# A ring of expert weights under attention's early memory, with raw w_out in it, and the row sums of the state-space half moved ahead

## The chip, the cores and the metric

The kernel runs on one core of a Trainium2 chip. The core has five engines that run at the same time, each with its own list of instructions: TensorE (matrix products), VectorE, ScalarE, GpSimd and SyncE (which here only issues transfers). The time is device microseconds of one execution; the median of several executions counts.

## The reference

One block of a streaming encoder on 1024 tokens of width 1024, all in float32. A combined input projection feeds a state-space mixer and a stick-breaking attention; both outputs are normed, joined and projected; a routed mixture of 32 experts follows.

```python
h = rms_norm(x, g_mix)
u, q, k, v = split(h @ w_in)                    # 512 columns each, 8 heads of 64
y_ssm = s5_mixer(u, ...)                        # ends with y * sigmoid(y @ w_glu + b_glu)
y_att = stick_breaking_attention(rms_norm(q, g_q), rms_norm(k, g_k), v)
mixed = concat(rms_norm(y_ssm, g_ssm_out), rms_norm(y_att, g_attn_out))
x = x + mixed @ w_out                           # w_out: 1024 x 1024
h2 = rms_norm(x, g_ffn)
x = x + hierarchical_moe(h2, ...)               # group top 1, expert top 2; gate, up, down per expert
```

The norms divide each token's row by the root of its mean square, so the joined projection needs the sum of squares of every token over the 512 columns of each half.

## The kernel before, in words

**Stages.** The input projection and the state-space scan are interleaved. Then comes attention, then the output projection with the router's logits, then the experts. The state-space output lies transposed in `yT` (columns on the partitions, tokens along the row); after its gate it is called `zT`, in the same memory. Attention writes its output, also transposed, over `q_t`, where it is called `oT`.

**Attention** (L672 to L756) is 64 steps: four pairs of heads, eight blocks of 128 queries each, two heads per block. `att_a` computes the scores on TensorE (L688, L689, L692), their sigmoid on ScalarE (L693), one minus it on GpSimd (L694) and a scan along the keys on VectorE (L697). `att_b`, three steps later, transposes the weights on TensorE (L708) and copies them to `aT` on ScalarE (L712) or VectorE (L714). `att_c` multiplies by `v_t` (L721) and copies the result to `oT` on ScalarE (L723). `sb`, `bb` and `aT` are the buffers in between. Queries and keys of a pair are prepared in one of two sets: set 0 for pairs 0 and 2, set 1 for pairs 1 and 3.

**The work list** (L725) spreads the state-space gate over attention: every third step takes one entry. `glu_w` loads and splits the gate's weights, `glu_split` splits half of `yT`, `glu_n` computes one block of the gate; the last multiplication is L660. With the last entry the pool of the GLU tiles is closed. `pair_prep` runs among these steps too.

**The seam.** After attention, `w_out` (1024 x 1024) is loaded in eight pieces of 512 KB into a buffer `wor` that is two deep (L794), scaled and split into a high part `wh` on ScalarE (L795) and a low part `wl` on VectorE (L796). `row_ss` (L800 to L817) takes the row sums of one half: for each 512 tokens, four squares on ScalarE (L806) and four products with a 128 x 32 matrix of ones on TensorE (L807), each into its own strip of 32 partitions of one bank, a copy (L809), four transposes (L812) and a reduction (L813); then the inverse root. It runs for `zT` and for `oT`, both after attention by the program, though the order of an engine's list may differ from it.

**The output projection** runs over eight tiles of 128 tokens. The left operand is split as well (`mh` L87, `ml` L88); each pair of parts gives three products (L91 to L93) of 128 x 128 by 128 x 512, 48 per tile. When a tile is done, its rows are normed and transposed for the router (L1012).

**Memory.** Tiles are placed in pools on the left or the right side of a partition's memory, one behind the other. A pool that opens where a closed one lay takes over its memory, and each tile waits until the last reader of the memory under it is done. The pools that matter here: `prp` (pair set 0), `glp` (GLU tiles), `atp` (`sb`, `bb`, set 1, `aT`), `kp` and `rga` and `wop` (the split `w_out`) on the right; `late` and `p3` on the left. `p3` holds the router's weights `wr` and biases `br_b`, `wor`, the squares, `mh`, `ml` and the x tiles. `br_b`, `wr` and `gpc` are loaded by transfers that ScalarE's queue issues (L778 to L785); SyncE issues the others.

**The experts' weights** come in units of 1 MB, which SyncE issues (L855) in order. A unit goes into the next place of `ring`: five places in `rga`, two in `q_t`, two in `yT`, and eight more that open later, 17 in all (`LK`). The first five are issued at the seam (L859), the sixth at tile 4 of the output projection. The matrix products of the experts are L1198, L1204, L1210, L1216 and L1228; a stop there with nothing else late is a wait for weights.

Of the kernel before, what the change touches and what calls it, by code (L numbers as in the profile page):

```python
# [8 lines left out]
F32 = mybir.dt.float32  # L9
# [3 lines left out]
AF = mybir.ActivationFunctionType  # L13
OP = mybir.AluOpType
AX = mybir.AxisListType
# [3 lines left out]
D = 1024  # L19
T = 1024  # L20
NT = 8
P = 128
# [9 lines left out]
def dram(ap, offset, pattern):  # L32
    return bass.AP(tensor=ap.tensor, offset=ap.offset + offset, ap=pattern)
# [3 lines left out]
def block_kernel(ctx, tc, x, g_mix, w_in, lam_re, lam_im, log_dt, b_re, b_im, c_re, c_im, d_skip,  # L37
                 w_glu, b_glu, g_q, g_k, g_so, g_ao, w_out, g_ffn, w_rg, b_rg, w_re, b_rexp,
                 w_gate, w_up, w_down, out, dbg=None, stop=99):
    nc = tc.nc  # L40
    mm = nc.tensor.matmul
# [3 lines left out]
    act = nc.scalar.activation  # L45
# [3 lines left out]
    mixp = ctx.enter_context(tc.tile_pool(name="mixp", bufs=1, side="left"))  # L49
# [20 lines left out]
    def bank(tag):  # L70
        return banks["pool"].tile([P, 512], F32, tag=tag, bufs=banks[tag], name=tag)

    def acc():
        return bank("acc")

    def trb():
        return bank("tr")
# [8 lines left out]
    def split(hi, lo, src):  # L86
        nc.scalar.copy(hi, src)  # L87
        tt(lo, src, hi.bitcast(F32), op=OP.subtract)  # L88
# [6 lines left out]
    ident = const.tile([P, P], F32, name="ident")  # L95
# [10 lines left out]
    for j, gsrc in enumerate((g_q, g_k)):  # L106
        for hf in range(2):
            nc.gpsimd.dma_start(gqk[64 * hf:64 * hf + 64, j:j + 1], dram(gsrc, 0, [[1, 64], [1, 1]]))
    negm = mixp.tile([P, P], BF, name="negm")
    nc.gpsimd.memset(negm, 0.0)  # L110
    nc.gpsimd.affine_select(out=negm, in_=negm, pattern=[[-1, P]], base=0, channel_multiplier=1,
# [517 lines left out]
    oT = [q_t[:, :, P * j:P * j + P] for j in range(4)]  # L629
    yTv = yT.rearrange("p k c t -> p k (c t)")  # L630
    zT = yTv
    glw = {}
# [12 lines left out]
    def glu_split(hf):  # L645
        yh = glp.tile([P, 4, 512], FR, name="yh", tag="yh")
        yl = glp.tile([P, 4, 512], FR, name="yl", tag="yl")
        split(yh, yl, yTv[:, :, 512 * hf:512 * hf + 512])
        glw["y", hf] = (yh, yl)

    def glu_n(hf, n):
        yh, yl = glw["y", hf]
        pg = acc()
        for k_ in range(4):
            ns = slice(n * P, (n + 1) * P)
            split_mm(pg, glw["gh"][:, k_, ns], glw["gl"][:, k_, ns], yh[:, k_], yl[:, k_], k_ == 0, k_ == 3)
        sg = glp.tile([P, 512], F32, name="sg", bufs=1)
        act(sg, pg, AF.Sigmoid, bias=glw["bg"][:, n:n + 1])
        hs = slice(512 * hf, 512 * hf + 512)
        tt(zT[:, n, hs], sg, yTv[:, n, hs], op=OP.mult)  # L660


    sbuf = [atp.tile([P, T], F32, name=f"sb{j}") for j in range(NB)]
    bbuf = [atp.tile([P, T], F32, name=f"bb{j}") for j in range(NB)]
# [51 lines left out]
    def att_c(pr, i):  # L716
        po = acc()
        for j in range(i + 1):
            for r in range(2):
# [4 lines left out]

    work = [glu_w] + [x_ for hf in range(2) for x_ in  # L725
                      [lambda hf=hf: glu_split(hf)] + [lambda hf=hf, n=n: glu_n(hf, n) for n in range(4)]]
    steps = [(h, i) for pr in range(4) for i in range(8) for h in (2 * pr, 2 * pr + 1)]
    LAG = 3
    nxt = None
    for n in range(len(steps) + LAG + 1):  # L730
        if n < len(steps):
            h, i = steps[n]
            att_a(h, i)
        if n > LAG:
            h, i = steps[n - LAG - 1]
            if h % 2:
                att_c(h // 2, i)
        if LAG <= n < len(steps) + LAG:
            att_b(*steps[n - LAG])
        if n % 3 == 0 and work:  # L740
            work.pop(0)()
            if not work:
                glu_s.close()
        if n < len(steps) and n % 16 == 4 and n // 16 < 3:
            nxt = pair_prep(n // 16 + 1)
        if n % 2 == 0 and nxt is not None:
            next(nxt, None)
    atp_s.close()
    qkvp.close()
    prp_s.close()  # L750
# [5 lines left out]


    kp = ctx.enter_context(tc.tile_pool(name="kp", bufs=1, side="right", reuse_waits="tile"))
    rga = ctx.enter_context(tc.tile_pool(name="rga", bufs=1, side="right", reuse_waits="tile"))
    late_s = ExitStack()  # L760
    late = late_s.enter_context(tc.tile_pool(name="late", bufs=1, side="left", reuse_waits="tile"))
    o3 = ExitStack()
# [2 lines left out]
    p3 = o3.enter_context(tc.tile_pool(name="p3", bufs=1, side="left", reuse_waits="tile"))  # L765
    h2d = drp.tile([T, D], F32, name="h2d")
    NE = 32
    NL = 4 + NE

    ring = [rga.tile([P, 2048], F32, name=f"rg{j}") for j in range(5)]  # L770
    ring += [q_t.rearrange("p t n -> p (t n)")[:, 2048 * j:2048 * j + 2048] for j in range(2)]
    ring += [yT.rearrange("p k c t -> p (k c t)")[:, 2048 * j:2048 * j + 2048] for j in range(2)]
    wo = [[wop.tile([P, D], FR, name=f"{nm}{c}") for nm in ("wh", "wl")] for c in range(8)]
# [2 lines left out]
    nc.sync.dma_start(gcat[:, 4:8], dram(g_ao, 0, [[1, P], [P, 4]]))  # L776
    wr = p3.tile([P, 8, NL], F32, name="wr")
    nc.scalar.dma_start(wr[:, :, 0:4], w_rg[0].rearrange("(p c) n -> p c n", c=8))  # L778
    nc.scalar.dma_start(wr[:, :, 4:NL], w_re[0].rearrange("(p c) g n -> p c (g n)", c=8))
    gpc = kp.tile([P, 8], F32, name="gpc")  # L780
    nc.scalar.dma_start(gpc, dram(g_ffn, 0, [[8, P], [1, 8]]))
    tt(wr, wr, gpc.unsqueeze(2).to_broadcast([P, 8, NL]), op=OP.mult)
    br_b = p3.tile([P, NL], F32, name="br_b")
    nc.scalar.dma_start(br_b[:, 0:4], dram(b_rg, 0, [[0, P], [1, 4]]))
    nc.scalar.dma_start(br_b[:, 4:NL], dram(b_rexp, 0, [[0, P], [1, NE]]))  # L785
    ones = late.tile([P, 32], F32, name="ones")
    nc.vector.memset(ones, 1.0)
    desc = late.tile([P, NE], F32, name="desc")
    nc.gpsimd.iota(desc, pattern=[[-1, NE]], base=NE, channel_multiplier=0,
                   allow_small_or_imprecise_dtypes=True)  # L790

    for c in range(8):
        raw = p3.tile([P, D], F32, name="wor", bufs=2)
        nc.sync.dma_start(raw, w_out[0, c * P:(c + 1) * P, :])  # L794
        act(wo[c][0], raw, AF.Copy, scale=gcat[:, c:c + 1])  # L795
        stt(wo[c][1], raw, gcat[:, c:c + 1], wo[c][0].bitcast(F32), op0=OP.mult, op1=OP.subtract)  # L796

    rs = [late.tile([P, NT], F32, name=f"rs{a}") for a in range(2)]

    def row_ss(a, src):  # L800
        ss = p3.tile([P, NT], F32, name="ssa", bufs=2)
        for hf in range(2):
            pq = acc()
            for k_ in range(4):
                sq = p3.tile([P, D], F32, name="sq3", tag="h2", bufs=2)[:, 0:512]
                act(sq, src(k_, hf), AF.Square)  # L806
                mm(pq[32 * k_:32 * k_ + 32, :], ones, sq, start=True, stop=True)  # L807
            sr = p3.tile([P, D], F32, name="sr3", tag="x2T")[:, 0:512]
            nc.scalar.copy(sr, pq)  # L809
            pt = trb()  # L810
            for t in range(4):
                nc.tensor.transpose(pt[:, t * P:(t + 1) * P], sr[:, t * P:(t + 1) * P], ident)  # L812
            nc.vector.tensor_reduce(ss[:, 4 * hf:4 * hf + 4],  # L813
                                    pt.rearrange("p (t k r) -> p t k r", t=4, k=4)[:, :, :, 0],
                                    op=OP.add, axis=AX.X)
        r = rstd_of(ss, 512, "ra", p3)
        nc.vector.tensor_copy(rs[a], r)  # L817

    row_ss(0, lambda k_, hf: zT[:, k_, 512 * hf:512 * hf + 512])
    row_ss(1, lambda k_, hf: oT[k_][:, 4 * hf:4 * hf + 4, :])  # L820


    LK = len(ring) + 8
# [19 lines left out]
    def load_units(n, eng=nc.sync):  # L843

        while loaded[0] < min(n, len(units)):
            k_ = loaded[0]
            ap, s_, rows, hf = units[k_]
            e = s_
            if s_ >= NF:
                if s_ not in ev_sp:  # L850
                    ev_sp[s_] = nc.values_load(evs[0][0:1, s_:s_ + 1], engines=[mybir.EngineType.SP],
                                               min_val=0, max_val=NE - 1)
                e = ev_sp[s_]
            t_ = ring[k_ % LK]
            eng.dma_start(t_.rearrange("p (c n) -> p c n", c=rows), wsrc(ap, e, hf, rows))  # L855
            raws[k_] = t_
            loaded[0] += 1

    load_units(5)  # L859


    NS = NE - NF
# [48 lines left out]
    side = kp.tile([P, 1], F32, name="side")  # L911
# [24 lines left out]
    def place(i, js):  # L936

        for j in js:
            mm(pr_[:, i, :] if i < NT - 1 else pr7[:, 0, :], tri if j == i else oneb, memb[:, j, :],
               start=j == 0, stop=j == i)  # L940
# [78 lines left out]
    def router_tile(i):  # L1019
        r, x2T = x2s[i]["r"], x2s[i]["x2T"]  # L1020
        pl = acc()
        for c in range(8):
            mm(pl[:, 0:NL], x2T[:, c], wr[:, c], start=c == 0, stop=c == 7)

# [50 lines left out]
    for i in range(NT):  # L1075
        out_open(i)
        out_part(i, 0, 0)
        out_part(i, 0, 1)
        if i:
            router_turn(i - 1)  # L1080
        out_part(i, 1, 0)
        if i:
            router_tile(i - 1)
            norm_store(i - 1)
            router_gates(i - 1)
        out_part(i, 1, 1)
        if i < NT - 1:
            out_close(i)
        if i == 4:
            load_units(6)  # L1090
        if i >= 2:
            place(i - 2, range(i - 1))
    place(NT - 2, range(NT - 2))
# [547 lines left out]
    with tc.For_i(0, nx, 1) as j:  # L1641
# [21 lines left out]
        for cg in range(2):  # L1663
            pt = pb("tr").rearrange("p (c t) -> p c t", c=4)
# [12 lines left out]
        pt = pb("tr").rearrange("p (c t) -> p c t", c=4)  # L1677
# [34 lines left out]
```

## Time and profile before

| | |
|---|---|
| runs | 1250.51, 1247.23, 1247.06 us |
| median | 1247.23 us |
| the profiled execution | 1249.28 us |
| its span in the profile | 1247.6 us |
| TensorE busy | 1091.5 us (87%) |
| VectorE, ScalarE, GpSimd busy | 635.3, 343.0, 255.6 us |
| attention's last copy starts | 448.30 us |
| first transposes for the router | 487.07 us |

All times within the execution are us from the start of its span; the profiled execution is 1.7 us longer than its span. An engine's busy time is the time in which one of its instructions ran; for TensorE the ends are modelled. "Granted clock" is the share of TensorE's full clock that the chip allowed in a stretch. "DMA share" is the mean busy share of the 16 transfer engines.

### The profile page before, as it was taken

Reading aid. Unit: us, or ns where it says so; the run is one execution under the profiler, and the core shown is the slowest. Engines: PE = TensorE matmul, PEld = TensorE weight load, DVE = VectorE, ACT = ScalarE, POOL = GpSimd, SP = SyncE. Lnnn points to the kernel's source line nnn. Section 1 sums busy time; section 2 is a strip of 40 time slices with the busy share of each in tenths; the row PEclk is TensorE's granted clock in tenths of the full one; section 3 lists DMA queues with packets and bytes.
Section 4 is the critical chain, followed back from the end, with each engine's and each line's share of the span. In section 5 each row is a group of like instructions: output and inputs, shape, how many; then the busy total and the mean of one; then the engine's idle time right before and its main releaser. Section 6 shows DMA issues by size and latency. Waiting matters only on the chain. (4 is left out here: it accounts for less than half of the span.)

```text
span 1247.6 us, 19611 instructions
## 1 busy us (share of the span) xinstructions
PE 1091.5 (87%) x6562; PEld 701.3 (56%) x6562; DVE 635.3 (51%) x1487; ACT 343.0 (27%) x656; POOL 255.6 (20%) x399
## 2 busy tenths in 40 slices
PE   5999999979998879997669978999789988899985
PEld 5999999966776637886334324444243443334432
DVE  6888777779788856656533221222332232321211
ACT  6225244366667654332101010010000010100011
POOL 4043122033334411221012021011210110211111
PEclk9999999989999999999789998999899998999988
DMA  7252322020001044345699998779998799998992
GB/s 250 85 104 45 63 67 68 19 85 18 2 1 55 19 165 175 134 152 219 229 367 318 382 393 296 290 240 377 388 397 326 240 363 395 358 392 313 364 400 44
DMA packets 95579, 268.15 MB, mean 215 GB/s; under 512 B 44308, under 2 KB 57432, under 8 KB 70840
## 3 DMA queue, kind: packets, MB, share of 16 engines
q1 hardware_dynamic: 80664, 232.29, 50.1%
q0 software_dynamic: 11232, 27.31, 8.9%
q10 hardware_dynamic: 3520, 6.46, 1.5%
q8 instruction: 93, 1.52, 0.5%
q14 instruction: 70, 0.57, 0.1%
HBM read 240.73 MB, written 24.12 MB: 212 GB/s over the span
## 5 line engine op out<-in xcount | busy, mean ns | idle before, releaser
L91 PE MATMUL acc<-wh,hTh 128*128 128x256 f32 x512 | 146.9, 287 | 4.1 <-ACT wh L87 4.1
L92 PE MATMUL acc<-wl,hTh 128*128 128x256 f32 x512 | 145.9, 285 | 0.0
L93 PE MATMUL acc<-wh,hTl 128*128 128x256 f32 x512 | 145.0, 283 | 0.0
L91 PEld LDWEIGHTS acc<-wh,hTh 128*128 128x128 f32 x512 | 97.6, 191 | 4.8 <-ACT wh L87 4.7
L92 PEld LDWEIGHTS acc<-wl,hTh 128*128 128x128 f32 x512 | 97.6, 191 | 0.7 <-DVE wl L88 0.6
L93 PEld LDWEIGHTS acc<-wh,hTl 128*128 128x128 f32 x512 | 97.6, 191 | 0.0
L697 DVE TENSOR_TENSOR_SCAN bb<-bb,sb 128x128 f32<-128x128 f32 (+7 forms) x64 | 89.9, 1419 | 12.7 <-POOL bb L694 12.1
L1183 POOL DMA_INDIRECT out_dram<-ysa,idx x23 | 35.1, 1524 | 295.8 <-DVE idx L1303 166.4
L1444 DVE TENSOR_TENSOR hs<-hs,acc 128x512 f32<-128x512 f32 x11 | 7.6, 688 | 153.4 <-ACT hs L1440 83.3
L694 POOL TENSOR_SCALAR bb<-sb 128x128 f32<-128x128 f32 (+7 forms) x64 | 63.9, 1001 | 96.7 <-ACT sb L693 87.0
L1183 POOL DMA_INDIRECT out_dram<-ysf,idx x13 | 20.5, 1574 | 199.4 <-ACTq L1378 82.5
L1204 PE MATMUL acc<-rw,xt 128*64 128x512 f32 x192 | 53.1, 668 | 6.9 <-issue 6.6
L1439 ACT ACTIVATE hs<-acc 128x512 f32<-128x512 f32 x11 | 6.6, 597 | 188.8 <-PEq L1378 78.1
L1198 PE MATMUL acc<-rg,xt 128*128 128x512 f32 x120 | 56.0, 613 | 1.2 <-DVEq L1378 0.9
L1198 PE MATMUL acc<-rw,xt 128*128 128x512 f32 x128 | 56.9, 592 | 0.0
L1188 PEld LDWEIGHTS tr<-ident,xga 128*128 128x128 f32 x256 | 32.3, 194 | 43.4 <-issue 32.5
L1188 PE MATMUL tr<-ident,xga 128*128 128x128 f32 x256 | 38.3, 295 | 18.2 <-DMA xga<-h2d,idx 9.8
L708 PE MATMUL tr<-ident,bb 128*128 128x128 f32 x288 | 45.8, 283 | 8.8 <-DVE aT L714 3.6
L91 PE MATMUL acc<-wh,mh 128*128 128x512 f32 x128 | 52.2, 411 | 0.0
L721 PE MATMUL acc<-aT,v_t 128*64 128x128 f32 x576 | 46.2, 281 | 5.7 <-DVE aT L714 4.7
L93 PE MATMUL acc<-wh,ml 128*128 128x512 f32 x128 | 50.7, 396 | 0.0
L92 PE MATMUL acc<-wl,mh 128*128 128x512 f32 x128 | 50.6, 396 | 0.0
(511 smaller groups left out, 2318.0 us busy)
## 6 DMA issues: line engine op xcount, KB each, us to landing
rw<-in_w_down_dram SPq DMA_DIRECT2D x28, 1024.0 KB
rw<-in_w_gate_dram SPq DMA_DIRECT2D x28, 1024.0 KB
rw<-in_w_up_dram SPq DMA_DIRECT2D x27, 1024.0 KB
rg<-in_w_gate_dram SPq DMA_DIRECT2D x20, 1024.0 KB
rg<-in_w_up_dram SPq DMA_DIRECT2D x20, 1024.0 KB
rg<-in_w_down_dram SPq DMA_DIRECT2D x20, 1024.0 KB
wraw<-in_w_in_dram SPq DMA_DIRECT2D x16, 512.0 KB
yT<-in_w_up_dram SPq DMA_DIRECT2D x8, 1024.0 KB
```

The source lines that it names most:

```text
L91: mm(o, ah, bh, start=first, stop=False)
L92: mm(o, ah, bl, start=False, stop=False)
L93: mm(o, al, bh, start=False, stop=last)
L694: nc.gpsimd.tensor_scalar(bt[:, off:T], st[:, off:T], -1.0, 1.0, op0=OP.mult, op1=OP.add)
L697: nc.vector.tensor_tensor_scan(rv, rv, sv, 0.0, op0=OP.mult, op1=OP.add)
L708: nc.tensor.transpose(pt[:, j * P:(j + 1) * P], st[:, off + (j0 + j) * P:off + (j0 + j + 1) * P], ident)
L721: mm(po[64 * r:64 * r + 64, :P], v_t[:, j, 64 * h:64 * h + 64], ATT["T", h, i][:, j, :], start=j == 0, stop=j == i)
L1183: nc.gpsimd.indirect_dma_start(out=rows, out_offset=bass.IndirectOffsetOnAxis(ap=idx[:n, :1], axis=0), in_=src[r], in_offset=None, compute ...
L1188: nc.tensor.transpose(pt[:, c], xg[:, 4 * cg + c::8], ident)
L1198: mm(p[j], xt[:, k_], hv[2 * (k_ // 4) + j][:, 512 * (k_ % 4):512 * (k_ % 4) + 512], start=k_ == 0, stop=k_ == 7)
L1204: mm(pg[r], xt[:, k_, LO], hv[2 * (k_ // 4) + j][:, 512 * (k_ % 4):512 * (k_ % 4) + 512], start=k_ == 0, stop=k_ == 7)
L1444: tt(hs, hs, pu, op=OP.mult)
```

## The change

The ring's own places move from the right side, where they lay over the memory that attention uses to its end, to the left side, ahead of `late` and `p3`, and there are six of them in place of five. The eight raw pieces of `w_out` are loaded into the halves of the ring's first four places instead of into `wor`. The pools behind the ring shift: `late` and `p3` come to lie further up on the left.

The row sums of the state-space half become two entries at the end of the work list, `z_sums(0)` and `z_sums(1)`, in attention's steps 33 and 36, with a small pool of their own. `ones` and the sums `ssz` move to a pool that is there from the start. The row sums of attention's half stay after attention. With six places of its own the ring has 18; six units are issued first, the seventh at tile 4.

```diff
+    ones = mixp.tile([P, 32], F32, name="ones")
+    nc.vector.memset(ones, 1.0)
+    ssz = mixp.tile([P, NT], F32, name="ssz")
...
+    def row_part(hf, src, ss, sq_tile, sr_tile):
+
+        pq = acc()
+        for k_ in range(4):
+            sq = sq_tile()
+            act(sq, src(k_), AF.Square)
+            mm(pq[32 * k_:32 * k_ + 32, :], ones, sq, start=True, stop=True)
+        sr = sr_tile()
+        nc.scalar.copy(sr, pq)
+        pt = trb()
+        for t in range(4):
+            nc.tensor.transpose(pt[:, t * P:(t + 1) * P], sr[:, t * P:(t + 1) * P], ident)
+        nc.vector.tensor_reduce(ss[:, 4 * hf:4 * hf + 4],
+                                pt.rearrange("p (t k r) -> p t k r", t=4, k=4)[:, :, :, 0], op=OP.add, axis=AX.X)
+
+    def z_sums(hf):
+        if hf == 0:
+            glw["zs"] = zs_s.enter_context(tc.tile_pool(name="zsp", bufs=1, side="right", reuse_waits="tile"))
+        zsp = glw["zs"]
+        row_part(hf, lambda k_: zT[:, k_, 512 * hf:512 * hf + 512], ssz,
+                 lambda: zsp.tile([P, 512], F32, name="sqz", bufs=2), lambda: zsp.tile([P, 512], F32, name="srz"))
...
+    work += [lambda: z_sums(0), lambda: z_sums(1)]
...
-            if not work:
+            if len(work) == 2:
                 glu_s.close()
...
-    rga = ctx.enter_context(tc.tile_pool(name="rga", bufs=1, side="right", reuse_waits="tile"))
+    rga = ctx.enter_context(tc.tile_pool(name="rga", bufs=1, side="left", reuse_waits="tile"))
...
-    ring = [rga.tile([P, 2048], F32, name=f"rg{j}") for j in range(5)]
+    NR = 6
+
+    ring = [rga.tile([P, 2048], F32, name=f"rg{j}") for j in range(NR)]
...
     for c in range(8):
-        raw = p3.tile([P, D], F32, name="wor", bufs=2)
+
+        raw = ring[c // 2][:, D * (c % 2):D * (c % 2) + D]
         nc.sync.dma_start(raw, w_out[0, c * P:(c + 1) * P, :])
...
-    row_ss(0, lambda k_, hf: zT[:, k_, 512 * hf:512 * hf + 512])
-    row_ss(1, lambda k_, hf: oT[k_][:, 4 * hf:4 * hf + 4, :])
+    row_rstd(0, ssz)
+    sso = p3.tile([P, NT], F32, name="sso")
+    for hf in range(2):
+        row_part(hf, lambda k_: oT[k_][:, 4 * hf:4 * hf + 4, :], sso,
+                 lambda: p3.tile([P, D], F32, name="sq3", tag="h2", bufs=2)[:, 0:512],
+                 lambda: p3.tile([P, D], F32, name="sr3", tag="x2T")[:, 0:512])
+    row_rstd(1, sso)
...
-    load_units(5)
+    load_units(NR)
...
-            load_units(6)
+            load_units(NR + 1)
```

## Rows read from the trace of the kernel before

**Rows 1.** Timeline of GpSimd and ScalarE, end of attention: start, duration, instruction, [idle before].
```profile
435.29 3.14 POOL L694 TENSOR_SCALAR bb<-sb 128x1024 f32<-128x1024 f32 x2 [2.51 <-ACT sb L693]
438.37 0.15 POOL L873 IOTA pcol<- 128x1 f32 x1
...
448.30 0.27 ACT L723 COPY q_t<-acc 128x128 f32<-128x128 f32 x1 [2.05 <-PE acc L721]
448.72 2.19 ACT L795 ACTIVATE wh<-wor,gcat 128x1024 fp32r<-128x1024 f32 x2 [0.15 <-issue]
```

**Rows 2.** Windows: length, busy us per engine, TensorE's granted clock, DMA share, GB/s.
```profile
370.00:380.00 10.00, 10.00 (x105) 8.10 (x99) 4.46 (x6) 6.66 (x18) 3.85 (x6) 1.00 0.01 2
380.00:390.00 10.00, 9.17 (x77) 7.22 (x76) 9.72 (x9) 8.65 (x20) 3.79 (x4) 1.00 0.00 0
...
400.00:410.00 10.00, 7.27 (x77) 5.85 (x78) 8.13 (x11) 4.38 (x11) 4.57 (x11) 1.00 0.73 222
...
450.00:460.00 10.00, 6.60 (x22) 1.80 (x22) 4.46 (x7) 7.69 (x12) 0.00 (x0) 1.00 0.73 270
460.00:470.00 10.00, 8.48 (x23) 2.81 (x24) 5.78 (x18) 6.77 (x11) 0.00 (x0) 0.83 0.73 244
```
In a window's line the five busy times are TensorE, its weight loads (PEld), VectorE, ScalarE and GpSimd.

**Rows 3.** Timeline of ScalarE's queue, 400 to 409 us.
```profile
402.61 0.55 ACTq L779 DMA_DIRECT2D wr<-in_w_router_expert_dram  x1
...
403.37 4.43 ACTq L784 DMA_DIRECT2D br_b<-in_b_router_group_dram  x1
```

**Rows 4.** Timeline of TensorE around the first transposes for the router.
```profile
485.66 0.40 PE L91 MATMUL acc<-wh,mh 128*128 128x512 f32 x1
...
487.07 1.05 PE L1012 MATMUL tr<-ident,xt 128*128 128x128 f32 x8
```

**Rows 5.** Groups, 448 to 487 us: count | busy us, mean ns | idle before, releasers.
```profile
L807 PE MATMUL acc<-sq,ones 128*32 128x512 f32 x32 | 13.7, 674 | 4.8 <-ACT sq L806 4.8
L796 DVE SCALAR_TENSOR_TENSOR wl<-wor,gcat,wh 128x1024 fp32r<-128x1024 f32 x8 | 10.3, 1282 | 5.9 <-ACT wh L795 5.9
...
L795 ACT ACTIVATE wh<-wor,gcat 128x1024 fp32r<-128x1024 f32 x8 | 9.1, 1145 | 3.3 <-DMA wor<-in_w_out_dram 3.2 <-issue 0.2
L806 ACT ACTIVATE sq<-q_t 128x512 f32<-128x512 f32 x8 | 4.7, 620 | 1.5 <-PE acc L807 1.5
...
L812 PE MATMUL tr<-ident,sr 128*128 128x128 f32 x16 | 2.6, 283 | 0.9 <-ACT sr L809 0.9
...
L807 PEld LDWEIGHTS acc<-sq,ones 128*32 128x32 f32 x32 | 2.2, 115 | 12.1 <-ACT sq L806 11.1 <-issue 0.9
```

**Rows 6.** Timeline of SyncE's queue: the first and the last pair of w_out loads.
```profile
398.55 1.89 SPq L794 DMA_DIRECT2D wor<-in_w_out_dram  x2
...
468.98 1.90 SPq L794 DMA_DIRECT2D wor<-in_w_out_dram  x2
```

**Rows 7.** Windows and TensorE's timeline in the experts' stage.
```profile
775.00:800.00 25.00, 23.04 (x89) 10.17 (x89) 6.42 (x15) 2.42 (x5) 2.37 (x2) 0.93 0.50 194
...
875.00:900.00 25.00, 17.12 (x94) 7.52 (x96) 10.12 (x25) 2.12 (x5) 6.83 (x5) 0.82 1.02 393
...
898.12 2.83 PE L1204 MATMUL acc<-rw,xt 128*64 128x512 f32 x6 [4.60 <-issue]
...
1067.29 3.47 PE L1204 MATMUL acc<-rw,xt 128*64 128x512 f32 x10 [2.01 <-issue]
```

**Rows 8.** Timeline of TensorE: a pair of ones products, and a lone one.
```profile
448.19 1.05 PE L807 MATMUL acc<-sq,ones 128*32 128x512 f32 x4
...
466.18 1.04 PE L807 MATMUL acc<-sq,ones 128*32 128x512 f32 x2
467.16 0.50 PE L91 MATMUL acc<-wh,mh 128*128 128x512 f32 x1
```

**Rows 9.** The low parts ml inside attention, 409 to 448 us: count, duration min/median/max.
```profile
L88 DVE TENSOR_TENSOR ml<-yT,mh x2: 683/806/928, 411.5 to 414.5; 128x512 fp32r<-128x512 f32 x2
L88 DVE TENSOR_TENSOR ml<-q_t,mh x2: 1115/1125/1135, 418.2 to 422.9; 128x512 fp32r<-128x512 f32 x2
```

More of the change, by code (lines that the diff above doesn't have):

```diff
@@ L660, in glu_n @@
         tt(zT[:, n, hs], sg, yTv[:, n, hs], op=OP.mult)
+    def row_part(hf, src, ss, sq_tile, sr_tile):
[11 more added lines that the diff above has]
+                                pt.rearrange("p (t k r) -> p t k r", t=4, k=4)[:, :, :, 0], op=OP.add, axis=AX.X)
+    zs_s = ExitStack()
+    def z_sums(hf):
[4 more added lines that the diff above has]
+                 lambda: zsp.tile([P, 512], F32, name="sqz", bufs=2), lambda: zsp.tile([P, 512], F32, name="srz"))
     sbuf = [atp.tile([P, T], F32, name=f"sb{j}") for j in range(NB)]
@@ L747, in block_kernel @@
             next(nxt, None)
+    zs_s.close()
     atp_s.close()
@@ L785, in block_kernel @@
     nc.scalar.dma_start(br_b[:, 4:NL], dram(b_rexp, 0, [[0, P], [1, NE]]))
-    ones = late.tile([P, 32], F32, name="ones")
-    nc.vector.memset(ones, 1.0)
     desc = late.tile([P, NE], F32, name="desc")
@@ L798, in block_kernel, with row_rstd @@
     rs = [late.tile([P, NT], F32, name=f"rs{a}") for a in range(2)]
[L800 to L815, printed above, removed]
+    def row_rstd(a, ss):
         r = rstd_of(ss, 512, "ra", p3)
         nc.vector.tensor_copy(rs[a], r)
-    row_ss(0, lambda k_, hf: zT[:, k_, 512 * hf:512 * hf + 512])
-    row_ss(1, lambda k_, hf: oT[k_][:, 4 * hf:4 * hf + 4, :])
+    row_rstd(0, ssz)
[5 more added lines that the diff above has]
+    row_rstd(1, sso)
     LK = len(ring) + 8
```

## The prediction

> **What bounds the kernel now.** I read the end of each stage in the timelines first, then the windows of the span for the limiting engine of each stretch, the groups of instructions between attention and router, the queues around that seam, and last what the experts wait for. The change touches three stretches.
>
> Attention ends with its last copy, which starts at 448.30 [rows 1]. Its late part is tight on two engines in turn: from 370 to 380 us TensorE is busy all 10.00 us and VectorE 4.46; from 380 on VectorE's scans fill 9.72 of 10 and TensorE 9.17. One stretch falls out: 400 to 410, with TensorE at 7.27 and ScalarE at 4.38 [rows 2]. ScalarE's queue says why: the issue of a 2 KB transfer for `br_b` held it for 4.43 us from 403.37 [rows 3].
>
> The seam runs from 448.3 to the first transposes for the router at 487.07 [rows 4], 38.8 us. TensorE is not its limit: 6.60 of 10 busy in one window, 8.48 in the next at a granted clock of 0.83, which stretches the busy time itself [rows 2]. The groups show ScalarE's list in its place, eight `wh`, six squares of `yT` and eight of `q_t` among it, and the weight loads of the ones products stood idle 12.1 us, 11.1 of it behind a square [rows 5]. SP issues the `w_out` loads two by two, the first pair at 398.55, the last at 468.98, since the buffer `wor` is two deep [rows 6]; ScalarE waits for them only 3.2 us [rows 5].
>
> In the experts TensorE works nearly without a gap (23.04 of 25 us from 775 to 800), until weights run out: in that window the places are full and DMA is down to 0.50; from 875 to 900 it is at 1.02, TensorE at 17.12 of 25, with one stop of 4.60 us at 898.12. Another, of 2.01 us, stands at 1067.29 [rows 7].
>
> **The change part by part.**
>
> *Row sums of the state-space half, into attention.* Eight ones products, eight squares, two copies, eight transposes and two small reductions join the work list for its steps 33 and 36, which fall near 370 to 380 us. A ones product shows as two records. Alone it took 1.04 us, two of them in different strips of a bank 1.05 together [rows 8]. So eight cost TensorE between 4.2 (all in pairs) and 8.3 us (all alone); the eight transposes add 1.3, half of the 2.6 for sixteen [rows 5]. ScalarE gets ten instructions of a square's size, 0.62 each, 6.2 us over 10 to 20 us in which it is used 6.66 of 10 [rows 2, 5]: it fits. VectorE's two reductions are nothing beside 4.46 of 10. TensorE has no cover there; its cover is what it idles in the window after, 0.83 us [rows 2], and the lag of three steps by which matmuls run ahead of the scans. Between 2 and 8 us; nearer to the paired price, since products of one half go to four strips one after another: +4.
>
> A rule speaks against this placing. What the rows show: behind the lone ones product at 466.18 the 128-wide projection product starts 0.98 us later [rows 8], so the switch of shape shows no gap beyond the product itself. The Trainium skill (TensorEngine Tiling (Array Packing), Tiling Modes) says that a change of tiling mode drains TensorE. By that rule the sums would not pair among attention's products and cost the upper price, +8, and the sum would be 1247, the end of the forecast's own range; the lone row shows no price above 1.04.
>
> *What leaves attention.* By the sizes and order of the allocations, the ring's six places of 8 KB per partition come to lie over pair set 0 and GLU tiles, `late` behind it, and pool `p3` behind that, over attention's `sb` and `bb`, which are in use nearly to the end. Before, `p3` lay over pair set 0 and the GLU tiles, and part of it ran inside attention. That a tile over live memory waits, with everything behind it on its engine, shows in pools that lay so before: GpSimd's first instruction for `kp` came at 438.37, right behind its last `bb`; ScalarE's first `wh` at 448.72, right behind attention's last copy, though its data had been asked for at 398.55 [rows 1, 6]. So the `br_b` issue and four `ml` (1.6 and 2.2 us on a full VectorE [rows 9]) leave. TensorE lost 2.73 us in the window of the issue [rows 2]; of the 3.8 us of `ml` I count two thirds, as TensorE's lag hides some. Together -5 (-3.5 to -6). Attention nets -1 (-4 to +2.5).
>
> *Raw `w_out` in the ring.* Eight loads of 512 KB go out near 398 instead of two; nothing that attention then runs reads from DMA, so it costs nothing. ScalarE's 3.2 us of waiting go. Six loads leave SP's queue in the seam, but expert units 0 to 3 now wait there until the raw halves in their places are split; the experts start over 100 us later, which hides it.
>
> *The seam.* Gone: half of the ones products and transposes (4.2 to 8.3 plus 1.3 us of TensorE) and six squares of `yT` (3.7 us of ScalarE). New: what `p3` kept in attention. ScalarE first issues five router transfers, 2.3 us at some 0.5 [rows 3], plus 0 to 4.4 if `br_b` stalls once more (I take 1.5), then eight `wh` (9.1), four `mh` of a square's size (2.5) and eight squares of `q_t` (4.9) [rows 5]. If the `wh` go first, tile 0's first product comes after 2.3 + 1.5 + 9.1 and about 1.5 for a first `mh` and `ml`: 14.4 us behind attention's end. Then 72 products of 0.235 (six from 485.66 to 487.07 [rows 4]): 16.9. The remaining ones products and transposes take 5.5 to 9.6, say 7, and the lower clock about 2. That is 40.3 against 38.8, and the x tiles load late too: +2 (-2 to +5).
>
> A second rule bears on the stall. The row has 4.43 us for one issue, and 0.55 for the one before it [rows 3]. The Trainium skill (DMA: Bandwidth & Descriptors, Issuing engines are not separate DMA queues) says that transfers of all issuers run on the same sixteen engines, and that the time of an issue is usually small. The stall is an exception to the second half; by the page alone the seam would be 1.5 us shorter and the sum 1241.5.
>
> *Eighteen places instead of seventeen.* One unit of 1 MB is 2.7 us of supply at the rate of the starved window, 393 GB/s [rows 7]. At both stops the weights can be that much earlier: 2.7 of the 4.60 and all of the 2.01, about -5 (-8, if the slow products behind the stops go too, to 0).
>
> **Sum:** -1 + 2 - 5 = -4, on the profiled execution's own 1249.28 (span 1247.6, 1.7 around it): 1245.3. That execution lies 2.05 above the median of the runs, 1247.23; against the median the sum is **1243**.
>
> **The rivals.**
>
> *Row sums stall attention (slower).* TensorE takes its list in order; each ones product waits for its square, with two square buffers ScalarE waits in turn, and sigmoids stand behind. In the seam 16 products cost 12.1 us of such idling beside their work [rows 5], 0.76 each. At that rate eight cost 6 more than 5.5 to 9.6 of work: 11.5 to 15.6 in place of 4, the sum +4 to +8, about 1252. It decides from 1 us per product on (+8, nothing gained); from 1.5 the kernel is slower. For it speaks a TensorE without idle time; against it, that attention's own products lie between.
>
> *The projection starts among the splits (faster).* If `p3` is not held to the end, tile 0's products follow each split at 1.28 us [rows 5]: start 2 to 4, eight splits 10.3, the 24 products left 5.6, sums 7: 25 to 27 instead of 38.8, so -12; with `ml` and `br_b` left in attention +4, places -5: about 1235. For it: only two engines' rows show such holding, not this pool's.
>
> *The place is worth nothing.* DMA is at 1.02 when TensorE starves [rows 7]; if the 18th unit only shifts the stop, -1 + 2 = +1: 1248. Against it speaks the window at 0.50 before, full places and idle queues, which one place more would have used.
>
> *It doesn't do what it says:* the raw loads wait for a late reader of GLU or pair-set memory, go out after attention, and the seam gets longer by their 11 us: 1254.
>
> **How the numbers follow.** About 0.3%, 3.7 us, is what a measurement of this kernel can tell from no change. Chances: forecast 0.35 (its own range 1239 to 1247, half of it below 1243.5), splits 0.22, place worth nothing 0.23, stalls 0.17, no early loads 0.03. Faster: 0.22 + 0.5 x 0.35 + 0.05 from the edge of the third = 0.45. Slower: 0.17 + 0.03 = 0.20. Same: the other 0.35. The range goes from just under the splits' value to that of the stalls, 1234 to 1252, and leaves out their far halves and the last case.
>
> **What would show it.** Right: attention's end between 444 and 451; no gap of 4 us on ScalarE near 405; eight `w_out` loads before 412; `wh` back to back behind the last copy and `p3`'s first tiles with them, not before; the router's first transposes 37 to 44 us behind attention; shorter stops near 898 and 1067. Wrong: `mh` or `br_b` inside attention; 1 us of idling ahead of each ones product there; a stop of 4 us or more in the experts as before.

## The result, and the profile after

The changed kernel takes 1264.88 us (median of four runs, 1263.23 to 1265.67) where the kernel before takes 1247.14 in the same comparison: 1.0122 times as long, interval 1.0095 to 1.0149. It is slower by 17.7 us; 1243 was forecast, with 1252 as the upper end. The profiled execution takes 1264.11 us, its span is 1262.3.

By stages, from the profiles (attention's two columns run from the scan of its step 32 to that of step 48, and from there to the last copy; the seam to the router's first transposes; then to the first expert product; then to the end of the span):

| kernel | step 32 at | 32 to 48 | 48 to end | seam | router | experts |
|---|---|---|---|---|---|---|
| before | 368.7 | 38.1 | 41.5 | 38.8 | 119.8 | 640.8 |
| changed | 366.4 | 47.7 | 41.2 | 40.9 | 120.0 | 646.1 |

Attention ends at 455.30 in place of 448.30 [rows 1], though its step 32 comes 2.3 us earlier in this execution. The scans, first of the kernel before and then of the changed one (VectorE's timeline, steps 32 and 48):

```profile
368.68 0.73 DVE L697 TENSOR_TENSOR_SCAN bb<-bb,sb 128x128 f32<-128x128 f32 x2
...
406.78 0.41 DVE L697 TENSOR_TENSOR_SCAN bb<-bb,sb 128x128 f32<-128x128 f32 x1
```

```profile
366.43 0.41 DVE L724 TENSOR_TENSOR_SCAN bb<-bb,sb 128x128 f32<-128x128 f32 x1
...
414.09 0.41 DVE L724 TENSOR_TENSOR_SCAN bb<-bb,sb 128x128 f32<-128x128 f32 x1
```

The whole of attention's loss, 9.6 us, lies between them. The windows of the changed kernel (columns as in [rows 2]):

```profile
370.00:380.00 10.00, 9.94 (x70) 5.51 (x68) 2.69 (x4) 6.39 (x15) 1.57 (x4) 1.00 0.01 2
380.00:390.00 10.00, 9.99 (x74) 6.60 (x70) 5.23 (x6) 5.85 (x14) 2.38 (x4) 1.00 0.00 0
...
410.00:420.00 10.00, 8.17 (x92) 7.04 (x93) 6.82 (x10) 3.23 (x9) 4.11 (x5) 1.00 1.01 402
...
460.00:470.00 10.00, 2.44 (x4) 0.36 (x4) 10.00 (x9) 10.00 (x14) 0.00 (x0) 0.50 0.68 230
```

From 380 to 390 VectorE is busy 5.23 us where it was 9.72 [rows 2], and TensorE 9.99: VectorE, which runs the scans, now has idle time while TensorE is full. From 460 to 470 it is the other way: ScalarE and VectorE are full, TensorE works 2.44 us at half its clock. The groups of the changed kernel's TensorE from 364 to 412 us hold the row sums:

```profile
L671 PE MATMUL acc<-sqz,ones 128*32 128x512 f32 x16 | 6.3, 604 | 0.0
...
L676 PE MATMUL tr<-ident,srz 128*128 128x128 f32 x8 | 1.3, 279 | 0.1
```

7.6 us of work, and no idle time ahead of a ones product. The windows of the whole stretch, from the scan of step 32 to that of step 48, first of the kernel before and then of the changed one:

```profile
368.68:406.78 38.10, 33.52 (x299) 25.88 (x299) 31.36 (x35) 25.91 (x59) 16.10 (x22) 1.00 0.19 56
```

```profile
366.43:414.09 47.66, 42.95 (x327) 28.52 (x327) 31.90 (x34) 31.70 (x70) 14.54 (x16) 1.00 0.18 63
```

TensorE's busy time grows by 9.4 us, and it idles as long as before: 4.6 us, then 4.7. So nearly all of the 9.6 us is busy time of TensorE, 7.6 of it in the records of the sums and the rest in those of attention's own products, whose ends are modelled.

The seam, ScalarE's timeline of the changed kernel:

```profile
455.30 0.27 ACT L750 COPY q_t<-acc 128x128 f32<-128x128 f32 x1 [2.05 <-PE acc L748]
...
457.40 0.44 ACTq L814 DMA_DIRECT2D br_b<-in_b_router_group_dram  x1
...
458.37 8.43 ACT L824 ACTIVATE wh<-rg,gcat 128x1024 fp32r<-128x1024 f32 x8 [2.80 <-DMA wr<-in_w_router_group_dram]
466.70 1.14 ACT L670 ACTIVATE sq<-q_t 128x512 f32<-128x512 f32 x2
```

and TensorE's:

```profile
467.37 2.44 PE L671 MATMUL acc<-sq,ones 128*32 128x512 f32 x4 [12.11 <-ACT sq L670]
...
476.56 0.49 PE L91 MATMUL acc<-wh,mh 128*128 128x512 f32 x1
```

All eight splits stand ahead of the first square, so TensorE idles 12.11 us. The `w_out` loads go out early as said (SyncE's timeline; before, [rows 6]):

```profile
404.60 5.80 SPq L823 DMA_DIRECT2D rg<-in_w_out_dram  x8
```

In the experts the stop of [rows 7] is there again, as long as before, some time after a window with the DMA share down to 0.49 (the window, then TensorE's timeline):

```profile
775.00:800.00 25.00, 25.00 (x59) 11.02 (x58) 1.99 (x4) 0.00 (x0) 1.77 (x1) 1.00 0.49 173
```

```profile
910.81 9.34 PE L1223 MATMUL acc<-rw,xt 128*64 128x512 f32 x32 [4.59 <-issue]
```

### The profile page after: what moved, and what is told of

Read it like the earlier page. It is cut to its first block, busy times and chain, and to the rows that moved or that the text cites. A ratio compares the mean times of both kernels' runs of the same rounds, so it can differ in the third digit from the quotient of the medians.

```text
span 1262.3 us, 19618 instructions
## 1 busy us (share of the span) xinstructions
PE 1100.7 (87%) x6562; PEld 704.4 (56%) x6562; DVE 631.4 (50%) x1487; ACT 343.3 (27%) x656; POOL 257.3 (20%) x399
## 5 line engine op out<-in xcount | busy, mean ns | idle before, releaser
L1217 PE MATMUL acc<-rg,xt 128*128 128x512 f32 x144 | 66.0, 614 | 0.9 <-DVEq L1397 0.9
L1217 PE MATMUL acc<-rw,xt 128*128 128x512 f32 x144 | 62.9, 593 | 0.3 <-PEq L1479 0.3
L1207 PEld LDWEIGHTS tr<-ident,xga 128*128 128x128 f32 x256 | 32.2, 194 | 42.6 <-issue 32.2
L1207 PE MATMUL tr<-ident,xga 128*128 128x128 f32 x256 | 38.2, 294 | 17.5 <-DMA xga<-h2d,idx 9.2
## 6 DMA issues: line engine op xcount, KB each, us to landing
rw<-in_w_down_dram SPq DMA_DIRECT2D x20, 1024.0 KB, 19.1
```

What stands on the lines that cost most here:

```text
L1207: nc.tensor.transpose(pt[:, c], xg[:, 4 * cg + c::8], ident)
L1217: mm(p[j], xt[:, k_], hv[2 * (k_ // 4) + j][:, 512 * (k_ % 4):512 * (k_ % 4) + 512], start=k_ == 0, stop=k_ == 7)
```

## The experiments

The stages of all kernels, as above; the ratio is to the kernel before on the same chip.

| kernel | ratio (interval) | 32 to 48 | 48 to end | seam | router | experts |
|---|---|---|---|---|---|---|
| sums after | 1.0107 (1.0039 to 1.0175) | 38.1 | 42.9 | 49.7 | 119.8 | 641.9 |
| sums only | 1.0055 (1.0028 to 1.0081) | 47.9 | 43.3 | 35.0 | 125.2 | 641.6 |
| 17 places | 1.0113 (1.0044 to 1.0182) | 47.6 | 41.2 | 40.9 | 120.0 | 641.8 |
| sums late | 1.0132 (1.0063 to 1.0200) | 47.5 | 42.8 | 41.6 | 119.9 | 643.0 |
| ones short | 0.9998 (0.9969 to 1.0028) | 42.7 | 42.8 | 35.9 | 119.8 | 632.1 |
| before, ones short | 0.9941 (0.9912 to 0.9969) | 38.2 | 42.6 | 34.9 | 119.5 | 643.3 |
| splits last | 1.0112 (1.0064 to 1.0161) | 47.7 | 41.1 | 38.7 | 120.0 | 638.4 |
| short and splits last | 1.0028 (0.9997 to 1.0060) | 42.7 | 41.0 | 37.8 | 119.8 | 637.2 |
| changed again | 1.0125 (1.0094 to 1.0156) | 47.7 | 42.9 | 41.4 | 120.0 | 642.9 |
| before, 16 places | 1.0020 (1.0004 to 1.0037) | 38.1 | 42.5 | 38.1 | 120.1 | 633.3 |
| before, short, 4 raw | 0.9986 (0.9958 to 1.0015) | 38.1 | 42.7 | 41.6 | 119.8 | 633.7 |
| before, br_b by SyncE | 0.9997 (0.9975 to 1.0019) | 38.1 | 40.3 | 38.5 | 120.0 | 646.1 |
| ones wide | one run | 46.2 | 41.0 | 39.4 | 119.6 | 648.7 |
| other bank | one run | 47.9 | 41.3 | 38.7 | 120.0 | 644.5 |

**Sums after.** `z_sums` leaves the work list; `row_part` runs for both halves behind attention.

```diff
-    work += [lambda: z_sums(0), lambda: z_sums(1)]
...
-    row_rstd(0, ssz)
...
+    for a, ss, src in ((0, ssz, lambda k_, hf: zT[:, k_, 512 * hf:512 * hf + 512]),
+                       (1, sso, lambda k_, hf: oT[k_][:, 4 * hf:4 * hf + 4, :])):
+        for hf in range(2):
+            row_part(hf, lambda k_: src(k_, hf), ss,
...
+        row_rstd(a, ss)
```

> The changed kernel with the row sums of the state-space half back behind attention; ring on the left, raw w_out in it and 18 places kept. Theory (the sums stall attention): attention's last copy comes at 444 to 449 us, 7 to 11 us earlier than in the changed kernel (455.3), and the seam to the router's first transposes grows by 3 to 6 us to 44 to 47, so the total is 1259 to 1263. Rival (the shifted pools, the 4 MB burst of loads and the new order cost attention): last copy still at 453 to 456, total 1266 or more. For the experts: if their extra 5 us come with 18 places, 645 to 647 us from the first expert product to the end; if from where TensorE's clock happens to fall, anywhere from 640 to 647.

Attention's stretch is back at 38.1 us, its end at 449.15: the sums, and neither the loads nor the shifted pools, cost the 9.6. The seam overshoots its 44 to 47: 49.7, 10.9 over the kernel before with the same work in it. That is the price of the ring's move with its early loads. The experts take 641.9 with 18 places, so their other 5 us did not come with the places. ScalarE's timeline, then TensorE's:

```profile
452.26 8.43 ACT L823 ACTIVATE wh<-rg,gcat 128x1024 fp32r<-128x1024 f32 x8 [2.84 <-DMA wr<-in_w_router_group_dram]
```

```profile
461.26 2.44 PE L671 MATMUL acc<-sq,ones 128*32 128x512 f32 x4 [12.14 <-ACT sq L670]
```

**Sums only.** The kernel before with `work += [z_sums(0), z_sums(1)]` and `row_part` for `oT`; ring, loads and places as before.

> The kernel before with nothing but the two entries of row sums moved into attention's work list. Theory (the sums stall attention): last copy at 454 to 459 us against 448.3, the seam shorter than 38.8 by 3 to 6 us, total 1248 to 1254. Rival (memory shift does it): last copy at 447 to 451, total 1241 to 1246.

47.9 us with the old memory too. The seam gets only 3.8 us shorter: with the sums gone, the next thing late is the raw data, whose two buffers SyncE fills in turn (waits, 458 to 500 us; kernel before: 3.2). The gain did not last. The router's stage got 5.4 longer, nearly all of it in its first 19.1 us (13.9 before), where TensorE has a granted clock of 0.82 against 1.00. The waits:

```profile
ACT wh L822 <- DMA wor<-in_w_out_dram: 10.7, 4, 3.9
```

**17 places.** `NR = 5` in place of 6.

> The changed kernel with five places in place of six in the ring's own memory, 17 in all. If the places are worth nothing: the experts take 640 to 647 us as in either kernel, and the stop of 4.6 us stays. If the 18th place pays, they take 2.5 to 5 us more than the changed kernel's 646. If 18 places cost (their order of loads), they take 640 to 642 and the total falls to 1258 to 1260. Attention's end stays at 454 to 456 by every theory.

Experts 641.8, where the two executions of the changed kernel have 646.1 and 642.9. That lies in the range of "worth nothing" and in that of "18 places cost"; the total, 1.0113, is as slow as with 18. The run alone does not decide; the other kernels with 18 places, 632.1 to 648.7, show that a difference of this size is within the spread.

**Sums late.** Two empty entries ahead of `z_sums` in the work list: steps 39 and 42.

> The changed kernel with the two entries of row sums six steps later, at steps 39 and 42, where VectorE's scans are the limit and TensorE idles 2 of 10 us. Theory (the sums cost where TensorE is full): attention ends 3 to 7 us earlier than in the changed kernel, 448 to 452, total 1257 to 1262. Rival (each ones product stalls ScalarE and the scans wherever it stands): 454 to 457, total 1263 to 1267.

The rival's side: 47.5 us. The last copy comes at 459.58, later than either said, since this execution reached step 32 later than the changed kernel's by 2.9 us and lost 1.6 more behind step 48. TensorE's idle tenths beside the scans were no room. With the sums among them it was busy 9.56 in a window where VectorE then had 6.41:

```profile
390.00:400.00 10.00, 9.56 (x48) 4.17 (x47) 6.41 (x6) 6.05 (x13) 1.67 (x2) 1.00 0.01 2
```

**Ones short.** The ones become a full matrix in the rounded type `float32r`, whose products are as short as the projection's, and the four squares of a half are summed in the bank.

```diff
-            mm(pq[32 * k_:32 * k_ + 32, :], ones, sq, start=True, stop=True)
+            mm(pq, ones, sq, start=k_ == 0, stop=k_ == 3)
```

> The changed kernel with the ones products in the short form: a full 128 x 128 ones matrix in the rounded float32 type, the four squares of a half summed in one bank, so each takes about the 0.235 us of a projection product in place of 0.52 to 1.04; squares, copies and transposes stay. Theory (TensorE's time for the sums is the price in attention, 7.6 us of it where it has none to spare): attention's last copy comes 4 to 6 us earlier, at 449 to 451, and the seam is 1 to 4 us shorter, total 6 to 10 us under the changed kernel. Rival (the waits are the price: ScalarE standing at its squares and copies, the sums' hold on one of two accumulator banks): last copy still at 453 to 456.

The stretch falls to 42.7, by 5.0, as the theory says. The last copy (454.12) lies in the rival's range all the same, since this execution reached step 32 later by 2.2 us and lost 1.6 more behind step 48. TensorE's groups, 364 to 412 us:

```profile
L669 PE MATMUL acc<-sqz,onesz 128*128 128x512 f32 x8 | 3.2, 438 | 0.0
L674 PE MATMUL tr<-ident,srz 128*128 128x128 f32 x8 | 1.3, 281 | 0.0
```

4.5 us of work, 4.6 us longer than in the kernel before: here the price is TensorE's time, and there is no more to explain. The seam gains 5.0.

**Before, ones short.** The same edit in `row_ss` of the kernel before.

> The kernel before with only the short form of the ones products. Theory: attention unchanged at 447 to 449; the seam loses 2 to 6 of its 38.8 us, total 2 to 6 us under the kernel before. Rival (the seam is paced by ScalarE's and VectorE's splits and not by the ones products): seam 38 to 40, no difference.

The seam loses 3.9 us, the ratio is 0.9941 (0.9912 to 0.9969), about 7 us where 2 to 6 were expected. This version beats both kernels.

**Splits last.** The loop over `wh` and `wl` is written behind `row_rstd(1, sso)`; the loads stay where they were.

> The changed kernel with the scaling and splitting of w_out written behind attention's row sums in the program, so that ScalarE's list begins the seam with squares; the raw loads stay early. Theory (the seam is long because eight splits stand ahead of the squares on ScalarE and TensorE idles 12 us): TensorE's first ones product within 5 us of attention's end in place of 12.1, seam 33 to 38 in place of 40.9. Rival (ScalarE's whole list, whatever its order, sets the seam): 40 to 42. Attention's end unchanged at 454 to 456.

TensorE's first ones product comes 3.78 us after its last attention product:

```profile
459.65 2.43 PE L671 MATMUL acc<-sq,ones 128*32 128x512 f32 x4 [3.78 <-ACT sq L670]
```

The seam is 38.7, just over the 38 claimed and under the rival's 40. ScalarE's list still takes three splits behind the first two squares (from 460.03). Of the 8.3 us less idling ahead of the sums 2.2 remain, because the last splits and the four `mh` now come late and TensorE idles again ahead of the projection, 2.97 us. Both sides were half right: the order matters, and behind it stands ScalarE's whole list.

**Short and splits last.** Both edits.

> The changed kernel with both: the short ones products and the splits behind the row sums. If the two prices are apart: attention's end at 449 to 451 and seam 31 to 37, total 10 to 18 us under the changed kernel, 1247 to 1254 on a chip where the kernel before takes 1247. Rival: no better than the better of the two alone.

Attention gains as in the short form (its end, 452.21, is still 1.2 us later than expected); the seam (37.8) is worse than with the short form alone (35.9). At 1.0028 (0.9997 to 1.0060) it is not better than the better of the two.

**Changed again.** The changed kernel once more.

> The changed kernel once more, for a second profile and on the same chip as the next three. If the experts' extra 5 us (646.1 against 640.8) belong to the change, they are 645 to 647 again; if they come from where TensorE's clock falls in one execution, anywhere from 632 to 646, as in the eight variants so far (17 places: 641.6, 641.8, 643.3; 18 places: 632.1 to 643.0). Attention's end 455 and the seam 41 in both cases, total 8 to 17 us over the kernel before.

47.7 again, experts 642.9. The last copy comes at 458.93 and not at 455, mostly from what lies ahead of step 32 and behind step 48. The kernel is 1.25% slower again.

**Before, 16 places.** `range(4)` for the ring's own places, and one unit less at the two early calls.

> The kernel before with four places in place of five in the ring's own memory, 16 in all. If a place is worth what was forecast (2.7 us at each stop for weights), the total is 3 to 6 us over the kernel before, and the stop of 4.6 us in the experts grows to about 7. If the stops are not waits for weights, the stop stays at 4.6 and the total within 2 us.

Two places fewer than the changed kernel, and the stop is what it was. The total is 0.2% over the kernel before (1.0004 to 1.0037), 0.5 to 4.6 us: between the two expectations, so a small price of a place is not excluded.

```profile
892.85 4.99 PE L1204 MATMUL acc<-rg,xt 128*64 128x512 f32 x16 [4.68 <-issue]
```

**Before, short, 4 raw.** Short ones products, `wor` four deep, 16 places.

> The kernel before with the short ones products, four buffers for raw w_out in place of two, and 16 places to make room. Theory (raw data that is there early puts the splits ahead of the squares in ScalarE's list, and TensorE waits): seam 35 to 39, no shorter than the 34.9 with the short products alone. Rival (the wait for raw data is a price of the seam): 30 to 33.

41.6, longer than either side said and 6.7 over the short form alone. With four raw pieces there early, ScalarE splits four ahead of the squares (its timeline, then TensorE's):

```profile
448.38 4.26 ACT L797 ACTIVATE wh<-wor,gcat 128x1024 fp32r<-128x1024 f32 x4 [0.21 <-DVE sided L917]
```

```profile
453.22 1.31 PE L809 MATMUL acc<-sq,ones 128*128 128x512 f32 x2 [4.69 <-ACT sq L808]
```

**Before, br_b by SyncE.** `nc.sync.dma_start` in place of `nc.scalar.dma_start` for `br_b`.

> The kernel before with the two transfers for br_b issued by SyncE and not by ScalarE. Forecast's step (the 4.43 us issue on ScalarE costs attention 2 to 3 us): last copy at 445 to 446.5. Rival (attention's stretch from pair 2 to pair 3 waits on its own short blocks, and the issue is hidden there): 447.5 to 449.

Last copy at 447.19, between the two; 1.2 us from step 48 on, in one execution, and no difference in the total. The window that had 7.27 for TensorE [rows 2] has 8.01 without the stall:

```profile
400.00:410.00 10.00, 8.01 (x84) 6.49 (x83) 9.23 (x13) 5.89 (x14) 5.95 (x11) 1.00 0.74 227
```

**Ones wide.** The full matrix of ones in plain float32, otherwise as the short form.

> The changed kernel with a full 128 x 128 ones matrix in plain float32, the four squares of a half summed in one bank: as wide as attention's own products, but as slow as the strips. From attention's step 32 to step 48 the kernel before takes 38.1 us, the changed one 47.7, the short form 42.7, while the sums keep TensorE busy 7.6 us in the changed kernel and 4.5 in the short form. If TensorE's time alone is the price: the stretch is longer than 38.1 by what its ones products and transposes are busy, 8 to 9 us, so 46 to 48. If the switch between strips and full-width products costs 2 us on top: the stretch is 38.1 plus the busy time with nothing on top, and with strips it stays 2 over. If the price is waiting of ScalarE and not TensorE's time: as the changed kernel, 47.7, whatever the busy time.

TensorE's groups from 364 us on:

```profile
L669 PE MATMUL acc<-sqz,onefz 128*128 128x512 f32 x16 | 7.6, 606 | 0.0
L674 PE MATMUL tr<-ident,srz 128*128 128x128 f32 x8 | 1.3, 279 | 0.0
```

8.9 us of work and 8.1 us longer: nothing on top. The strips had 7.6 of work and cost 9.6. It is one execution, but the stretch is steady: 38.1 to 38.2 in all six kernels without sums in it, 47.5 to 47.9 in all with strips.

**Other bank.** `pq = trb()` in `row_part`.

> The changed kernel with the ones products written to a bank of the transposes' three and not to one of the two accumulator banks, which attention's own products then have for themselves. If the hold on an accumulator bank is the 2 us by which attention grows over TensorE's busy time: 45 to 46.5 us from step 32 to step 48. If it is not: 47 to 49.

47.9, again in one execution: the accumulator banks are not the 2 us.

## Why the prediction was wrong, point by point

**The row sums in attention: +4 forecast, +9.6 measured.** The step that failed is the cover. The +4 is the paired price, 5.5, less some 1.5 us that an idle 0.83 us of the next window and "the lag of three steps" were to pay. They paid for nothing: TensorE idles 4.6 to 4.7 us in the stretch with the sums and without them, and the stretch grew by what TensorE was busy longer. It is 47.5 to 47.9 us in every kernel with strips, at whichever steps they stood; in the short form 4.5 us of work cost 4.6. The pairing was also too hopeful. Two pairs formed and four products stood alone (TensorE's timeline, the first of each):

```profile
369.27 1.05 PE L671 MATMUL acc<-sqz,ones 128*32 128x512 f32 x4
...
371.48 1.04 PE L671 MATMUL acc<-sqz,ones 128*32 128x512 f32 x2
```

So the work was 7.6 us, inside the bounds (5.5 to 9.6) but not at their lower end. The rival had the sign and came nearer (11.5 to 15.6), but not by its mechanism: it let each product wait 0.76 us for its square, and the rows show 0.0 idle ahead of them. The 0.76 came from the idle time of weight loads, 12.1 us; the products themselves idled 4.8 [rows 5]. And of the range "Attention nets -1 (-4 to +2.5)" the upper end does not follow from its terms, which give 8 - 3.5 = +4.5.

About two of the 9.6 us are not in the records of the sums. Wide products show none of them, another bank leaves them, and the lone row from which I took "no gap beyond the product" [rows 8] could not show them. The Trainium skill (TensorEngine Tiling (Array Packing), Tiling Modes) says that a change of tiling mode drains TensorE; the strips among full-width products fit that, and I was wrong to set the rule aside on one row. But it is not shown to be the cause: in the wide form the four products of a half also ran back to back, so their grouping may share in it. VectorE's two reductions, which I put at nothing, are another candidate: VectorE stood idle 6.1 us ahead of them, waiting for their transposes, with scans behind (2.4 us in the short form). Neither was tried apart.

**What leaves attention: -5 forecast, nothing left of it at the end.** That `br_b` and the `mh` and `ml` leave attention was right, and it paid for a while: from step 48 to step 59 the changed kernel takes 20.4 us in both executions, the kernel before 22.8. Then step 60 comes 4.2 and 4.5 us later in place of 2.6. TensorE worked 2.25 of the 4.5 us before, and its granted clock fell, where the kernel before keeps 1.00 (windows of the changed kernel):

```profile
430.00:434.50 4.50, 2.25 (x24) 1.64 (x23) 4.50 (x4) 1.65 (x5) 2.36 (x2) 0.96 0.00 0
434.50:439.00 4.50, 4.50 (x23) 3.36 (x24) 2.29 (x4) 3.00 (x7) 0.95 (x1) 0.67 0.00 0
```

From step 48 to the end it takes 41.2 and 42.9 us, the kernel before 41.5. The failed step is that I read a gap in TensorE's busy time as a loss, all of which would come back at attention's end. The `br_b` stall, counted with 2.73, was worth 1.2 us in the one profile of the kernel before without it, and the window stays low without it (8.17 from 410 to 420 in the changed kernel). Attention goes from pair 2 to pair 3 there; that its short blocks wait for one another is my reading of the rest. The `ml` were not tried alone.

**The seam: +2 forecast, +2.1 measured, by other terms.** That the size came out is luck. That `p3` is held to attention's end was right (the five transfers start at 455.31, the `mh` behind the splits), and so was ScalarE's order. But the sum let tile 0's first product come 14.4 us behind attention and gave 25.9 us to what follows; it came after 21.3, with the ones products ahead of it, and what follows took 19.7. In the runs the ring's move costs 10.9 us, and taking half the sums away gives back 8.8. The first comes from an order, which the sum had no term for: with all raw data there, the splits stand ahead of the squares, and TensorE has nothing to do for 12.11 us. Four raw pieces early did the same to the kernel before. What follows then runs at half clock: the first two ones products took 2.44 us, in a window with a granted clock of 0.50 (1.2 of 2.4 GHz), against 1.05 for a pair [rows 8]. The Trainium skill (TensorE: Matmul & The Clock Gate, Part 1: The HAM clock gate) tells that TensorE falls to half its clock after an idle gap; the trace agrees, with 0.50 behind the 12.11 us.

**Eighteen places: -5 forecast, nothing gained at the stops.** The failed step is the reading of the stops in [rows 7] as waits for weights. The first of them is 4.53 to 4.85 us in every kernel, with 16, 17 or 18 places. The list of TensorE's waits in the experts of the kernel before (us in total, times, longest) has next to nothing behind a load of weights:

```profile
PE acc L1204 <- issue: 6.6, 2, 4.6
...
PE y L1216 <- DMA rg<-in_w_down_dram: 0.4, 1, 0.4
```

The trace says what "issue" is at the first stop. The sequencer of TensorE's list (PEldq) is in a branch there, as long in the kernel before as in the changed one (count, then ns min/median/max, then first and last start):

```profile
L1366 PEldq COMPARE_BRANCH  x2: 70/2712/5355, 884.2 to 892.5; - x2
```

```profile
L1385 PEldq COMPARE_BRANCH  x2: 70/2712/5355, 896.9 to 905.2; - x2
```

All sixteen traces have this branch, with 5.25 to 5.60 us; the median of a kernel's 225 branches is 0.21. The wait for the signal of the weights' load behind it took 0.05 us. Within each of these branches the transfer queue q8, whose kind the profile calls "instruction", moved one packet of 16 KB (DMA of the kernel before, 892.5 to 897.8 us: packets, MB, share):

```profile
q8 instruction: 1, 0.02, 1.3%
```

That packet ends at 896.42, 1.4 us before the branch does. At the second stop, which is no branch and stands in the middle of a group of products, another ends 1.3 us before TensorE goes on; the changed kernel has that stop too, 1.75 us at 1082.17. So I read both as waits for the engine's own instructions, which one place more in the ring did not shorten. Why the packets come so late no run settles, and where the 0.5 to 4.6 us of the kernel with 16 places sit its profile does not show: its experts took 633.3 us.

**The experts' other 5 us.** The changed kernel's first profile has 646.1 in the experts, the kernel before 640.8. That difference is not shown to belong to the change: the same experts' code with 17 places took from 640.8 to 646.1, with 18 from 632.1 to 648.7, and the changed kernel itself 642.9 the second time. In the profile all of it is TensorE's busy time for the same number of records, at a slightly lower granted clock (windows of the experts, before and changed):

```profile
606.83:1247.50 640.67, 556.66 (x2520) 243.07 (x2520) 178.76 (x448) 55.41 (x118) 91.52 (x71) 0.95 0.90 329
```

```profile
616.19:1262.30 646.11, 562.45 (x2520) 245.46 (x2520) 178.61 (x448) 55.39 (x118) 92.64 (x71) 0.94 0.89 326
```

So of 17.7 us the runs explain the 9.6 in attention and 2.1 to 2.6 in the seam. Of the rest I cannot say where it sits. The second comparison gave the same 1.25%, so it is more than the spread of single executions, but the profiles do not place it.

## What to carry to other kernels

Work put beside an engine that is full costs its own time, and a lag or an idle tenth elsewhere is no cover until a variant shows it; a window's idle share between dependent short steps is latency, not room. Data that arrives earlier can reorder the list of the engine that uses it, and what then stands behind may be what another engine lives on: ask who starves while the early data is worked on. A stop beside a busy DMA need not be a wait for the data: look in the list of waits, and at what the sequencer does, before paying for memory. Before paying to move work, make it shorter: the same products in a shorter form took 0.6% off the kernel before, with nothing moved.

## What the runs showed of the hardware that was not expected

Ones products in strips of 32 columns among full-width ones cost 9.6 us for 7.6 of busy time of their own, full-width ones 8.1 for 8.9. The issue of the small `br_b` transfer took 4.43 us on ScalarE with other loads under way [rows 3], and 0.44 in the changed kernel behind attention. One branch of TensorE took 5.25 to 5.60 us in each of sixteen kernels, with one packet of instructions moved meanwhile, where the median branch takes 0.21. And the experts took 632 to 649 us over the sixteen profiles, with TensorE busy 549 to 563 us for the same 2520 records at a mean granted clock from 0.96 down to 0.94.
